# Seven products instead of eight for one more couple of the second mixer's output pair, its weight sums made by VectorE

## The chip, the cores and the metric

The kernel runs on one core of a Trainium2 chip. The metric is device time in microseconds (us), the median of several executions; the profile is one further execution, recorded on the chip. The engines are TensorE (PE, with PEld for its weight loads), VectorE (DVE), ScalarE (ACT), GpSimd (POOL) and SyncE (SP), which here issues nearly all DMA transfers.

## What is computed

A two-layer encoder trunk on 256 tokens of width 2048, all in float32. Each layer is a token mixer and a gated MLP, each behind an RMS norm and added to the residual. The last step of each mixer is a 2048 by 2048 projection; the second mixer's is the one that the change touches:

```python
def hgrn_mixer(hn, w_in, lb, head_g, w_out):
    b, s, _ = hn.shape
    p = hn @ w_in
    ...
    y = head_rmsnorm(y, head_g, B_HEADS) * jax.nn.silu(g)
    return y @ w_out
...
for layer in range(DEPTH):
    hn = rmsnorm(h, norm_mix_g[layer])
    ...
    h = h + mix
    h = h + conv_glu(rmsnorm(h, norm_ffn_g[layer]), ...)
return rmsnorm(h, final_g)
```

## The kernel before

**Precision and products.** Every float32 operand is split in two: a rounded part (wh for weights, the left half of an activation tile) and the rest (wl, the right half). A product of two operands is three matmuls, high by high, high by low and low by high. For weights, ScalarE makes wh by a cast (L146) and VectorE makes wl by a subtraction (L147); both come from a raw tile that SP loads. Weight parts have four buffers each (WB) and, in some stages, two more in another pool (MORE), which every third piece takes by a running counter (`turns["w"]`). An engine works strictly in the order in which its instructions stand, and a scheduler sets that order when the program is built.

**Output projection.** The output of a mixer has four column blocks of 512. `mixed` makes the first (c0), then the two middle ones together (the pair, `two`), then the last (c3). The pair has 16 row tiles of weights, taken two by two: eight couples u = 0 to 7. A couple is a 2 by 2 block product: two halves of the tokens, two row tiles, two column blocks.

**Eight or seven products.** A plain couple needs eight block products, 24 matmuls of 128x512, which accumulate in four banks named pc. A couple in the list SEVEN_MIX is done with seven products (Strassen's scheme in Winograd's form), 21 matmuls, some of which accumulate in four more banks, named mm. That takes four sums of the activations (`token_sums`: tiles f and sx, made by VectorE at L652 and L546, split at L547 and L548) and four sums of the weights (a tile T of 128x1536, and a quarter that is put back into the raw tile). The list is (2, 4, 6) for both mixers.

**Where the weights' sums come from.** In the first mixer they are made on the fly: `combine` issues four VectorE subtractions of 128x512 (L206) one couple ahead. In the second mixer they are made much earlier, while TensorE works on the mixer's input projection, stored to memory (tscr) and loaded back as T (L197) and the last quarter of raw (L198). The tile T has two buffers in a pool that opens only when the mixer's heads are done, since it takes over the heads' memory.

**Order around the change.** The generator `split_squares` yields the pieces of a couple; `squares_by_seven` fetches them some pieces ahead and issues the matmuls; `token` makes the activations' sums of all listed couples as a side job. The mixer's last head is still being finished when the pair begins: its transposes (pz, L1104) are the last readers of the heads' memory.

In the names below, raw_16719 holds couple 1's weights (its halves become wh_16721 and wh_16757), raw_16761 and T_16763 belong to couple 2, and sx_16779 are couple 2's activation sums. yb0 to yb15 are the row tiles of the activations.

Of the kernel before, what the change touches and what calls it, by code (L numbers as in the profile page):

```python
# [8 lines left out]
F32 = mybir.dt.float32  # L9
# [6 lines left out]
P = 128  # L16
T = 256
D = 2048
KT = D // P
# [30 lines left out]
SEVEN = (2, 3, 4, 5, 6, 7, 8, 9), (1, 2, 3, 4, 5, 6, 7)  # L50
# [1 line left out]
SPLIT = (0, 2, 5), (0, 2, 5)  # L52
END = 3
SCRATCH = 4096
SEVEN_MIX = (2, 4, 6)

QUAD = 32
TMS = (0, 4, 8, 11, 15, 18, 21)
# [6 lines left out]
def trunk_kernel(ctx, tc, xT, x_d, fg_d, pp_d, cst_d, w_gate, w_first, w_aq, w_ak, w_av, w_ao, w_aout, w_ao2,  # L65
                 w_bq, w_bv, w_bg, w_bout, w_bo2, w_up, w_d0, w_d1, w_d3, out, mscr, tscr):
    nc = tc.nc
# [114 lines left out]
    def temporary(pool_, name):  # L182
        ff = pool_.name == "ff"
        return pool_.tile([P, 1536], F32, tag="avc" if ff else name, bufs=TEMP if ff else 2, name=name)
# [202 lines left out]
    class Norm:  # L387
# [73 lines left out]
        def x(self, k):  # L461
            side.until(lambda: self.xs[k] is not None)
            return self.xs[k]
# [59 lines left out]
    def project(wsrc, nk, x, norm):  # L523

        def done(c):
            def f_(ps):
                for t in range(2):
                    h = hm[:, t, 512 * c:512 * c + 512]
                    dve.tensor_tensor(h, h, ps[t], ALU.add)
                if norm is not None:  # L530
                    norm.add(c)
            return f_
        return [Chunk("tm", wsrc(c), nk, x, done(c)) for c in range(4)]
# [6 lines left out]
    def token_sums(mp, i, a, b, S, last=None):  # L540

        m = 384 if last else 512
        sx = mp.tile([P, 2 * m], F32R, tag=f"sx{i}", name="sx")
        for i, (x, y, op) in enumerate(((a[:, P:T], b[:, P:T], ALU.add), (a[:, P:T], a[:, 0:P], ALU.subtract),
                                        (S[:, 0:P], a[:, 0:P], ALU.subtract), (b[:, 0:P], S[:, 2 * P:3 * P], ALU.subtract))):
            dve.tensor_tensor(S[:, i * P:(i + 1) * P], x, y, op)  # L546
        act.copy(sx[:, 0:m], S[:, 0:m])  # L547
        dve.tensor_tensor(sx[:, m:2 * m], S[:, 0:m], sx[:, 0:m].bitcast(F32), ALU.subtract)  # L548
        if last:
            act.copy(last[0], S[:, m:512])  # L550
            dve.tensor_tensor(last[1], S[:, m:512], last[0].bitcast(F32), ALU.subtract)
        return [(sx[:, i * P:(i + 1) * P], sx[:, m + i * P:m + (i + 1) * P]) for i in range(m // P)] + ([last] if last else [])

    def pair(src, nk, c0, x, sums, norm, seven):

        def part(t, c):
            o = 512 * (c0 + c)
            return hm[:, t, o:o + 512]

        def mid(ps):  # L560
            P1, P6, P7, P5 = ps
            u = ev.tile([P, 512], F32, tag="jk", bufs=1, name="u")
            act.copy(u, P1)
            dve.tensor_tensor(part(0, 0), part(0, 0), P1, ALU.add)
            dve.tensor_tensor(u, u, P6, ALU.add)
            dve.tensor_tensor(part(0, 1), part(0, 1), P5, ALU.add)
            dve.tensor_tensor(part(0, 1), part(0, 1), u, ALU.add)
            dve.tensor_tensor(part(1, 1), part(1, 1), P5, ALU.add)
            dve.tensor_tensor(u, u, P7, ALU.add)  # L569
            pool.tensor_tensor(part(1, 0), part(1, 0), u, ALU.add)  # L570
            pool.tensor_tensor(part(1, 1), part(1, 1), u, ALU.add)

        def done(ps):
            for c in range(2):
                for t in range(2):
                    h = part(t, c)
                    dve.tensor_tensor(h, h, ps[2 * t + c], ALU.add)
                if norm is not None and c == 0:
                    norm.add(c0)
            if norm is not None:  # L580
                side.push(second())

        def second():
            yield 3.0
            norm.add(c0 + 1)

        ch = Chunk("st", src, nk, x, done)
        ch.mid, ch.seven, ch.sums = mid, seven, sums
        ch.stored, ch.waits, ch.pool, ch.ends, ch.rest = {}, (), None, False, False
        return ch  # L590
# [29 lines left out]
    early = ([], []), ([], [])  # L620
# [6 lines left out]
    def store(ch, src, u, todo):  # L627
        ch.stored[u] = tscr[turns["t"]]
        turns["t"] += 1
        todo.append((src[:, 2048 * u:2048 * (u + 1)], ch.stored[u]))  # L630

    def mixed(w, w2, x, norm, close, layer=None):

        c0, _, _, c3 = project(lambda c: w[c // 3], KT, x, norm)
        op, SX, first = ExitStack(), {}, c0.done

        def sums(u):
            side.until(lambda: u in SX)
            return SX[u]

        two = pair(w2, KT, 1, x, sums, norm, SEVEN_MIX)
        if layer is not None:
            for u in SEVEN_MIX:
                store(two, w2, u, early[layer][0])
            two.waits = [early[layer][1]]

        def token():
            for i, u in enumerate(SEVEN_MIX):
                f = temporary(two.pool, "f")
                for j in range(2):  # L650
                    y = x(2 * u + j).bitcast(F32)
                    dve.tensor_tensor(f[:, j * T:(j + 1) * T], y[:, 0:T], y[:, T:2 * T], ALU.add)  # L652
                SX[u] = token_sums(two.pool, i, f[:, 0:T], f[:, T:2 * T], f[:, 2 * T:4 * T])
                yield 5.0

        def done(ps):
            side.drain()
            close()
            two.pool = op.enter_context(tc.tile_pool(name="op", bufs=1))
            two.pool.tile([P, LEAD], F32, name="lead")  # L660
            first(ps)
            side.push(token())

        c0.done, c3.before = done, op.close
        return [c0, two, c3]


    def mlstm(norm, nxt):
# [270 lines left out]
        def yx(k):  # L939
            side.until(lambda: YT[k] is not None)  # L940
            return YT[k]

        return chunks + mixed(w_aout, w_ao2, yx, nxt, stack.close)


    def hgrn(norm, nxt):
# [196 lines left out]
        def yx(k):  # L1143
            side.until(lambda: YT[k] is not None)
            return YT[k]

        return chunks + mixed(w_bout, w_bo2, yx, nxt, stack.close, 1)


# [182 lines left out]
def build(nc, ins, out_shape=(2, P, D), **kw):  # L1332
    ap = {k: nc.dram_tensor("in_" + k, a.shape, mybir.dt.from_np(a.dtype), kind="ExternalInput").ap()
          for k, a in ins.items()}
    out = nc.dram_tensor("out", out_shape, F32, kind="ExternalOutput").ap()
    mscr = nc.dram_tensor("mscr", (64, T), F32, kind="Internal").ap()
    tscr = nc.dram_tensor("tscr", (len(SEVEN_MIX) + 4 * len(SEVEN[0]) + 4 * len(SEVEN[1]), P, 2048), F32, kind="Internal").ap()
    with tile.TileContext(nc, schedule_with_timeline_sim=True) as tc:  # L1338
        with ExitStack() as ctx:
            trunk_kernel(ctx, tc, ap["xT"], ap["x"], ap["fg"], ap["pp"], ap["cst"], ap["w_gate"], ap["w_first"],  # L1340
                         ap["w_aq"], ap["w_ak"], ap["w_av"],
                         ap["w_ao"], ap["w_aout"], ap["w_ao2"], ap["w_bq"], ap["w_bv"], ap["w_bg"],
                         ap["w_bout"], ap["w_bo2"], ap["w_up"], ap["w_d0"], ap["w_d1"], ap["w_d3"], out, mscr, tscr, **kw)
# [12 lines left out]
```

## Time and profile before

| | us |
|---|---|
| median of three runs | 2373.69 (2372.8 to 2375.37) |
| profiled execution, its own time | 2372.06 |
| its span, first to last instruction | 2370.1 |
| TensorE busy | 2357.5 |
| VectorE busy | 1965.9 |
| ScalarE busy | 1464.1 |
| second mixer's pair, first to last matmul of line 234 | 1600.6 to 1644.2 |

In a timeline a row merges equal instructions that follow each other: start, length of all, engine, line, operation, tiles, count, and in brackets the idle time just before with the instruction that ended it. Matmuls overlap in the pipeline, so the distance from one start to the next is shorter than the listed length of one. The granted clock of TensorE is 0.999 over the span.

### The profile page before, as it was taken

Reading aid. Unit: us, or ns where it says so; the run is one execution under the profiler, and the core shown is the slowest. Engines: PE = TensorE matmul, PEld = TensorE weight load, DVE = VectorE, ACT = ScalarE, POOL = GpSimd, SP = SyncE. Lnnn points to the kernel's source line nnn. Section 1 sums busy time; section 2 is a strip of 40 time slices with the busy share of each in tenths; the row PEclk is TensorE's granted clock in tenths of the full one; section 3 lists DMA queues with packets and bytes.
Section 4 is the critical chain, followed back from the end, with each engine's and each line's share of the span. In section 5 each row is a group of like instructions: output and inputs, shape, how many; then the busy total and the mean of one; then the engine's idle time right before and its main releaser. Section 6 shows DMA issues by size and latency. Waiting matters only on the chain. (4 is left out here: it accounts for less than half of the span.)

```text
span 2370.1 us, 38326 instructions
## 1 busy us (share of the span) xinstructions
PE 2357.5 (99%) x14548; PEld 2019.1 (85%) x14548; DVE 1965.9 (83%) x3028; ACT 1464.1 (62%) x2321; POOL 196.9 (8%) x244
## 2 busy tenths in 40 slices
PE   9999999999999999999999999999999999999998
PEld 8888888888888888888888888888888888888886
DVE  7777687888888898887887888778789888888988
ACT  7655456555565555675777777776555566555565
POOL 0100000000000000000232322220000000000000
PEclk9999999999999999999999999999999999999999
DMA  8776656888988888986666666646788898888896
GB/s 302 237 245 244 214 194 208 295 286 292 317 316 321 308 282 294 351 309 223 211 204 213 218 217 210 207 171 232 265 301 281 293 337 317 288 295 296 318 347 219
DMA packets 121832, 632.96 MB, mean 267 GB/s; under 512 B 13728, under 2 KB 14240, under 8 KB 77232
## 3 DMA queue, kind: packets, MB, share of 16 engines
q1 hardware_dynamic: 119952, 626.51, 75.0%
q0 software_dynamic: 1120, 3.21, 0.8%
q8 instruction: 114, 1.87, 0.3%
q10 hardware_dynamic: 576, 0.79, 0.1%
q14 instruction: 70, 0.57, 0.1%
HBM read 562.24 MB, written 68.22 MB: 266 GB/s over the span
## 5 line engine op out<-in xcount | busy, mean ns | idle before, releaser
L346 PE MATMUL mm<-xt,wh 128*128 128x512 f32 x3776 | 1311.6, 394 | 1.5 <-issue 1.5
L147 DVE TENSOR_TENSOR wl<-raw,wh 128x1024 fp32r<-128x1024 f32 (+1 forms) x844 | 1036.5, 1232 | 247.6 <-ACT wh L146 239.6
L146 ACT CAST wh<-raw 128x1024 fp32r<-128x1024 f32 (+1 forms) x844 | 876.1, 1043 | 528.8 <-PE mm L346 311.3
L350 PE MATMUL mm<-xt,wl 128*128 128x256 f32 x3776 | 1043.0, 278 | 0.0
L346 PEld LDWEIGHTS mm<-xt,wh 128*128 128x128 f32 x3776 | 705.5, 188 | 161.6 <-issue 1.8
L350 PEld LDWEIGHTS mm<-xt,wl 128*128 128x128 f32 x3776 | 709.2, 188 | 5.1 <-issue 0.4
L362 PE MATMUL mm<-wh,xt 128*128 128x512 f32 x1024 | 322.5, 393 | 0.8 <-ACT xt L368 0.6
L234 PE MATMUL pc<-wh,g 128*128 128x512 f32 x776 | 261.9, 390 | 0.0
L362 PEld LDWEIGHTS mm<-wh,xt 128*128 128x128 f32 x1024 | 191.5, 188 | 40.2 <-ACT xt L368 1.1
L611 DVE TENSOR_TENSOR praw<-praw 128x512 f32<-128x512 f32 x252 | 174.8, 694 | 43.7 <-DMA praw<-in_w_d 26.0
L362 PE MATMUL mm<-wl,xt 128*128 128x512 f32 x512 | 198.2, 391 | 0.0
L234 PEld LDWEIGHTS pc<-wh,g 128*128 128x128 f32 x776 | 145.6, 188 | 30.5 <-ACT wh L146 0.2
L234 PE MATMUL pc<-wl,g 128*128 128x512 f32 x388 | 151.0, 389 | 0.0
L234 PE MATMUL mm<-wh,sx 128*128 128x512 f32 x396 | 140.4, 389 | 0.0
L147 DVE TENSOR_TENSOR wl<-T,wh 128x1024 fp32r<-128x1024 f32 (+1 forms) x132 | 126.5, 969 | 12.3 <-ACT wh L146 12.1
L146 ACT CAST wh<-T 128x1024 fp32r<-128x1024 f32 (+1 forms) x132 | 109.6, 836 | 35.9 <-PE mm L234 13.1
L570 POOL TENSOR_TENSOR hm<-hm,u 128x512 f32<-128x512 f32 x10 | 14.8, 1482 | 1221.5 <-DVE u L569 1121.3
L362 PEld LDWEIGHTS mm<-wl,xt 128*128 128x128 f32 x512 | 96.2, 188 | 18.8
L1046 DVE TENSOR_TENSOR QK<-QK,G 128x256 f32<-128x256 f32 x224 | 104.7, 516 | 6.1 <-ACT kq L1025 5.7
L1170 ACT COPY avc<-mm 128x256 f32<-128x256 f32 x172 | 63.9, 372 | 65.8 <-PE mm L350 65.5
L1025 ACT COPY kq<-QK 128x512 f32<-128x512 f32 x112 | 74.5, 669 | 35.7 <-DVE QK L1046 27.8
L234 PEld LDWEIGHTS mm<-wh,sx 128*128 128x128 f32 x396 | 74.3, 188 | 15.4
(237 smaller groups left out, 2218.4 us busy)
## 6 DMA issues: line engine op xcount, KB each, us to landing
raw<-in_w_up SPq DMA_DIRECT2D x172, 1024.0 KB, 6.2
tscr<-praw SPq DMA_DIRECT2D x126, 512.0 KB, 6.7
praw<-in_w_d SPq DMA_DIRECT2D x120, 512.0 KB, 7.1
raw<-in_w_bq SPq DMA_DIRECT2D x48, 1024.0 KB, 5.0
T<-tscr SPq DMA_DIRECT2D x63, 768.0 KB, 8.1
raw<-in_w_d SPq DMA_DIRECT2D x60, 768.0 KB, 6.7
raw<-in_w_ao SPq DMA_DIRECT2D x24, 1024.0 KB, 4.8
raw<-in_w_d SPq DMA_DIRECT2D x24, 1024.0 KB, 7.4
```

Source lines behind the costliest of these rows:

```text
L146: pin(act.copy(wh[:, :m], r))
L147: pin(dve.tensor_tensor(wl[:, :m], r, wh[:, :m].bitcast(F32), ALU.subtract))
L234: pin(pe.matmul(ps, a, b, start=id(ps) not in begun, stop=stop and i == 2))
L346: pe.matmul(ps[f], wh[:, c:c + P], x, start=k + kk == 0, stop=False)
L350: pe.matmul(ps[f][:, 0:T], wl[:, c:c + P], x[:, 0:T], start=False, stop=k + kk == ch.nk - 1)
L362: pe.matmul(ps[t], x[:, a + t * P:a + (t + 1) * P], w[:, c], start=st and i == 0, stop=sp and i == 2)
L570: pool.tensor_tensor(part(1, 0), part(1, 0), u, ALU.add)
L611: dve.tensor_tensor(out, x, y, ALU.subtract)
L1025: act.copy(m, blocks(QK, h))
L1046: dve.tensor_tensor(two[:, j], two[:, j], by[:, j], ALU.mult)
L1170: act.copy(z, p[:, T:2 * T])
```

## The change

The second mixer's list becomes (2, 3, 4, 6); the first mixer's stays. Couple 3 is not stored early: it is named in FLY_MIX, so `combine` makes its weights' sums with VectorE during the pair, as all couples of the first mixer do. The scratch tensor gets one more slot, which nothing uses.

```diff
-SEVEN_MIX = (2, 4, 6)
+SEVEN_MIX = (2, 4, 6), (2, 3, 4, 6)
+FLY_MIX = (3,)
...
         op, SX, first = ExitStack(), {}, c0.done
+        seven = SEVEN_MIX[layer or 0]
...
-        two = pair(w2, KT, 1, x, sums, norm, SEVEN_MIX)
+        two = pair(w2, KT, 1, x, sums, norm, seven)
         if layer is not None:
-            for u in SEVEN_MIX:
-                store(two, w2, u, early[layer][0])
+            for u in seven:
+                if u not in FLY_MIX:
+                    store(two, w2, u, early[layer][0])
             two.waits = [early[layer][1]]

         def token():
-            for i, u in enumerate(SEVEN_MIX):
+            for i, u in enumerate(seven):
```

The program up to the second mixer's pair is the same instruction for instruction on every engine. From the pair on the scheduler orders the engines anew. Line numbers of the changed kernel are higher by one to three.

On ScalarE, this is the queue at the pair's second and third couple before, from the cast of couple 1's first half on (raw_16866 is couple 3's raw tile):

```order
L146 COPY wh_16721<-raw_16719 128x1024
L368 ACTIVATE yb15_16676<-pz_16673,pp_70 128x256
L146 COPY wh_16757<-raw_16719 128x1024
L146 COPY wh_16804<-T_16763 128x1024
L146 COPY wh_16868<-raw_16866 128x1024
L146 COPY wh_16766<-raw_16761 128x1024
L515 ACTIVATE jk_16745,ss8_16744<-hm_75 128x512
L547 COPY sx_16779<-f_16776 128x512
```

And this is the same place in the changed kernel (raw_16804 is now couple 3's raw tile):

```order
L147 COPY wh_16721<-raw_16719 128x1024
L369 ACTIVATE yb15_16676<-pz_16673,pp_70 128x256
L147 COPY wh_16811<-T_16763 128x1024
L147 COPY wh_16873<-raw_16804 128x1024
L147 COPY wh_16757<-raw_16719 128x1024
L147 COPY wh_16766<-raw_16761 128x1024
L147 COPY wh_16815<-raw_16761 128x1024
L516 ACTIVATE jk_16745,ss8_16744<-hm_75 128x512
L548 COPY sx_16779<-f_16776 128x512
```

The cast of couple 1's second half, wh_16757, was first after yb15; it now stands behind the cast of T_16763, which has to be loaded first, and behind a cast for couple 3. The cast of the activation sums sx_16779 moved back by one cast of weights too.

On TensorE, this is the place where couple 1's second half is first used, before:

```order
L234 MATMUL pc_16756<-wh_16687,yb1_11555 128x512
L234 MATMUL pc_16753<-wh_16757,yb3_12367 128x512
L234 MATMUL pc_16754<-wh_16757,yb2_12063 128x512
L234 MATMUL pc_16755<-wh_16757,yb3_12367 128x512
L234 MATMUL pc_16756<-wh_16757,yb2_12063 128x512
L234 MATMUL pc_16753<-wl_16758,yb3_12367 128x512
L234 MATMUL pc_16753<-wh_16757,yb3_12367 128x512
```

The same place in the changed kernel:

```order
L235 MATMUL pc_16756<-wh_16687,yb1_11555 128x512
L235 MATMUL pc_16753<-wh_16757,yb3_12367 128x512
L235 MATMUL pc_16754<-wh_16757,yb2_12063 128x512
L235 MATMUL pc_16755<-wh_16757,yb3_12367 128x512
L235 MATMUL pc_16756<-wh_16757,yb2_12063 128x512
L235 MATMUL mm_16749<-wh_16766,yb4_13286 128x512
L235 MATMUL mm_16750<-wh_16811,sx_16779 128x512
L235 MATMUL mm_16750<-wl_16812,sx_16779 128x512
L235 MATMUL mm_16751<-wh_16811,sx_16779 128x512
L235 MATMUL mm_16751<-wl_16812,sx_16779 128x512
L235 MATMUL mm_16752<-wh_16815,sx_16779 128x512
L235 MATMUL pc_16753<-wl_16758,yb3_12367 128x512
```

Up to the four matmuls with wh_16757 nothing moved; behind them six matmuls of couple 2, five of which use sx_16779, now come ahead of those with wl_16758.

On VectorE, between the rest of yb15 and wl_16758 stood only six small sums of f and the two additions to hm. Now two subtractions of couple 3 (L207), wl_16812, wl_16874, a third subtraction and the like number of small sums stand between them, and one subtraction of couple 3 stands ahead of yb15, so that all four come before wl_16758. Behind wl_16758 follow wl_16767, wl_16816 and then the rest of sx_16779.

On SP, the load of couple 4's T now stands behind three more transfers and waits until T_16763 is used up, since couple 3's own sums take the second buffer of T. Because the running counter of weight pieces is two higher after the pair, the second layer's MLP pairs put other pieces in the two additional buffers, and the scheduler orders them a little differently too; the number of operations there is the same.

More of the change, by code (lines that the diff above doesn't have):

```diff
@@ L1336, in build @@
     mscr = nc.dram_tensor("mscr", (64, T), F32, kind="Internal").ap()
-    tscr = nc.dram_tensor("tscr", (len(SEVEN_MIX) + 4 * len(SEVEN[0]) + 4 * len(SEVEN[1]), P, 2048), F32, kind="Internal").ap()
+    tscr = nc.dram_tensor("tscr", (len(SEVEN_MIX[1]) + 4 * len(SEVEN[0]) + 4 * len(SEVEN[1]), P, 2048), F32, kind="Internal").ap()
     with tile.TileContext(nc, schedule_with_timeline_sim=True) as tc:
```

## Prediction

> **What bounds the kernel now.** I read the page first, then the waits of TensorE, then the timelines of the second mixer's pair. On the page, the line of busy times says that TensorE has nearly no idle time to lose:
>
> ```profile
> PE 2357.5 (99%) x14548; PEld 2019.1 (85%) x14548; DVE 1965.9 (83%) x3028; ACT 1464.1 (62%) x2321; POOL 196.9 (8%) x244
> ```
>
> All waits of TensorE in the span, longest first (us in total, times, longest):
>
> ```profile
> PE mm L346 <- issue: 1.5, 1, 1.5
> PE idle L1239 <- POOL ones L1232: 1.1, 1, 1.1
> PE mm L362 <- ACT xt L368: 0.6, 1, 0.6
> PE pc L234 <- DVE wl L147: 0.4, 1, 0.4
> ```
>
> The span of 2370.1 us is TensorE's work, 3.6 us of waits and an end behind the last matmul. A change can gain only by taking matmuls away, and any new wait of TensorE is paid in full, since no later wait is there to swallow it. The one wait in line 234 lies in the pair that is changed. TensorE's timeline there:
>
> ```profile
> 1607.22 0.62 PE L362 MATMUL mm<-wh,yb 128*128 128x512 f32 x2
> ...
> 1608.81 1.36 PE L234 MATMUL pc<-wh,yb 128*128 128x512 f32 x5
> 1610.53 0.50 PE L234 MATMUL pc<-wl,yb 128*128 128x512 f32 x1 [0.36 <-DVE wl L147]
> 1610.86 0.39 PE L234 MATMUL pc<-wh,yb 128*128 128x512 f32 x1
> ...
> 1618.60 1.07 PE L234 MATMUL pc<-wh,yb 128*128 128x512 f32 x4
> 1619.51 0.39 PE L234 MATMUL mm<-wh,yb 128*128 128x512 f32 x1
> ```
>
> Four matmuls from 1618.60 to 1619.51 make 0.228 us for one from start to start. The five from 1608.81 are the last with couple 1's first half and the four with its second, wh_16757, so those four start at 1608.81 + 0.23 = 1609.04; the wait behind them is for wl_16758.
>
> **What the change takes away.** Couple 3 goes from 24 matmuls to 21: 3 times 0.228 is 0.68 us less on TensorE. It lies on the path, so all of it counts. That is the whole gain: 0.03% of the time, where about 0.2% (4.75 us) is what a measurement of this kernel can tell from no change.
>
> **What it adds, as work.** VectorE's rows in the pair and, for the subtractions of weights, in the first mixer's pair:
>
> ```profile
> 332.05 0.68 DVE L206 TENSOR_TENSOR T<-raw 128x512 f32<-128x512 f32 x1
> 332.65 1.22 DVE L147 TENSOR_TENSOR wl<-raw,wh 128x1024 fp32r<-128x1024 f32 x1
> ...
> 1604.66 1.43 DVE L652 TENSOR_TENSOR f<-yb 128x256 f32<-128x256 f32 x4 [2.94 <-PE pz L1104]
> 1606.01 0.28 DVE L546 TENSOR_TENSOR f<-f 128x128 f32<-128x128 f32 x1
> 1606.22 0.48 DVE L369 SCALAR_TENSOR_TENSOR yb<-pz,pp,yb 128x256 fp32r<-128x256 f32 x1
> 1606.61 1.09 DVE L546 TENSOR_TENSOR f<-f 128x128 f32<-128x128 f32 x5
> 1607.65 0.69 DVE L529 TENSOR_TENSOR hm<-hm,mm 128x512 f32<-128x512 f32 x1
> 1608.25 0.29 DVE L546 TENSOR_TENSOR f<-f 128x128 f32<-128x128 f32 x1
> ...
> 1611.69 2.36 DVE L147 TENSOR_TENSOR wl<-raw,wh 128x1024 fp32r<-128x1024 f32 x2
> ...
> 1635.30 2.36 DVE L147 TENSOR_TENSOR wl<-raw,wh 128x1024 fp32r<-128x1024 f32 x2 [3.56 <-ACT wh L146]
> ```
>
> From start to start a 128x512 operation takes 0.60 us (332.05 to 332.65), a sum of f from yb 0.34 (four in 1.35), a small sum 0.21, a wl of 1024 columns 1.14 (2.36 less one of 1.22). So VectorE gets four subtractions (2.4), two f (0.7), four small sums (0.8), the rest of sx (0.6) and the wl of T, 1.14 and about 0.6: 6.2 us. ScalarE gets casts of T, 0.96 and some 0.5, and of sx, some 0.5. Against this stands VectorE's free time by stages (us; busy PE, PEld, DVE, ACT, POOL; clock, DMA):
>
> ```profile
> 323.50:351.50 28.00, 28.00 (x125) 23.21 (x124) 26.52 (x33) 17.95 (x22) 0.00 (x0) 1.00 0.57 196
> 1604.60:1631.80 27.20, 26.84 (x119) 21.73 (x118) 25.93 (x41) 18.84 (x25) 0.00 (x0) 1.00 0.78 279
> 1631.80:1635.30 3.50, 3.50 (x17) 2.92 (x16) 0.00 (x1) 1.09 (x2) 0.00 (x0) 1.00 0.89 304
> ```
>
> In the first 27.2 us VectorE has 1.3 us free, then it idles through 3.5 us, because it ran ahead: 4.8 us for 6.2. By the sum alone TensorE would end up 1.4 us late. The first mixer's pair, in the first row, does three couples on the fly at 26.5 of 28.0 us with TensorE at 28.0 of 28.0. I take nothing for the work, because the wait worked out next gives VectorE more time than it lacks.
>
> **What it moves: the term that decides.** ScalarE at this place:
>
> ```profile
> 1604.66 0.47 ACT L368 ACTIVATE yb<-pz,pp 128x256 fp32r<-128x256 f32 x1 [4.20 <-PE pz L1104]
> 1607.87 1.06 ACT L146 CAST wh<-raw 128x1024 fp32r<-128x1024 f32 x1 [2.73 <-PE mm L362]
> 1609.47 1.05 ACT L146 CAST wh<-T 128x1024 fp32r<-128x1024 f32 x1 [0.55 <-DMA T<-tscr]
> 1610.43 2.00 ACT L146 CAST wh<-raw 128x1024 fp32r<-128x1024 f32 x2
> 1612.33 0.62 ACT L515 ACTIVATE jk<-hm 128x512 f32<-128x512 f32 x1
> ...
> 1612.95 0.60 ACT L547 CAST sx<-f 128x512 fp32r<-128x512 f32 x1
> ```
>
> And the transfer it waits for: SP's row, and the time to landing of the three loads of T in this pair (least, median, most); then the medians of raw loads of the same size here, and of all loads of T:
>
> ```profile
> 1604.71 0.80 SPq L197 DMA_DIRECT2D T<-tscr  x2
> ...
> DMA to landing us min/median/max: 4.7/6.1/6.1
> ...
> raw<-in_w_bo SPq DMA_DIRECT2D x3, 768.0 KB, 4.3
> ...
> T<-tscr SPq DMA_DIRECT2D x63, 768.0 KB, 8.1
> ```
>
> Today wh_16757 is cast at 1607.87, as soon as TensorE frees its buffer, ends at 1608.93, and TensorE takes it at 1609.04. In the new order the cast of T_16763 stands ahead of it. That tile's load cannot be issued before 1604.71: it waits for the head's transposes, which end there, and nothing of that changes. It lands 4.7 us later, so ScalarE stands still until 1609.47 with wh_16757, wh_16766, wh_16815 and sx_16779 queued behind.
>
> Then, with 0.96 us from cast to cast (1609.47 to 1610.43): T 1609.47, couple 3's raw 1610.43, wh_16757 1611.39, ended at 1612.44. TensorE waits from 1609.04 to about 1612.49, which is 3.45 us. Its four matmuls last until 1613.40; wh_16766 (started 1612.35) ends at that time, and its one matmul runs until 1613.68. The next needs sx_16779: wh_16815 starts at 1613.31, the squares of hm (L516) at 1614.27, sx 0.62 later at 1614.89, ending at 1615.49. TensorE goes on at 1615.54, a second wait of 1.86 us. That is the sixth matmul from 1609.04 on; the sixth starts today at 1610.86, with the 0.36 us wait ahead of it, which goes since wl_16758 is wanted later. So TensorE is 4.68 us later.
>
> Is VectorE ready by then? From 1604.66: two f, a subtraction, two f, a small sum, yb15 (0.39) and a small sum end at 1607.43; a subtraction, three small sums, two hm, a subtraction and two small sums at 1610.88; wl_16812 and wl_16874 at 1613.16, a subtraction and a small sum at 1613.97. So wl_16758 ends at 1615.19. TensorE wants it five matmuls after 1615.54, at 1616.68: 1.5 us in hand. The rest of sx_16779, three wl later, ends at 1618.1 and is wanted some four us after that. yb15 comes 0.6 us later than now, 0.1 us late for c0's last matmuls; the wait that follows swallows it.
>
> The sum: 4.68 less 0.68 is 4.0 us. The profiled execution took 2372.06 us (2370.1 of span and 2.0 around it), which makes 2376.1. The median of the runs shown, 2373.69, is 1.6 above that execution, so I forecast 2377.7. Only the landing of T is uncertain here, and it enters one to one: by the raw loads, 4.3 us, the change costs 3.6; by the other two of T, 6.1 us, 5.4. I take 4.7, because it is the same transfer released by the same matmul. The median of all loads, 8.1, is from stages with more traffic.
>
> **Rivals.** (1) No new wait: the cast of T does not hold up wh_16757, for instance because the two loads of T shared the engines and one alone lands much sooner. Only the 0.68 us would remain, 2373.0. It would take a landing by about 1606, 1.3 us after issue, and the least shown is 4.3.
>
> (2) The waits let TensorE's clock fall. In these rows the last matmul starts at 2360.93 and lasts 0.39, and the clock column then goes from 1.00 to 0.50; the row with 1.5 us of TensorE idle, around 1226, keeps 1.00:
>
> ```profile
> 2360.93 0.39 PE L234 MATMUL pc<-wh,g 128*128 128x512 f32 x1
> ...
> 1226.00:1228.00 2.00, 0.54 (x4) 0.22 (x3) 1.46 (x6) 1.70 (x6) 0.00 (x0) 1.00 0.77 320
> 2364.00:2366.00 2.00, 0.00 (x0) 0.00 (x0) 1.11 (x2) 1.03 (x2) 0.00 (x0) 0.80 0.37 136
> 2366.00:2368.00 2.00, 0.00 (x0) 0.00 (x0) 0.00 (x0) 0.00 (x0) 0.00 (x0) 0.50 1.03 371
> ```
>
> A mean of 0.80 says the fall came 1.2 us into 2364 to 2366, so 3.9 us after the last matmul ended. The new wait, about 3.3 us without a matmul running, lies between 1.5 and 3.9, nearer to the upper. If the clock falls and takes as long to come back as it took to fall, half of 3.9 us of matmuls is lost: 1.9 us, 2379.6. [...]
>
> (3) A second wait later in the pair. Couple 4's T is now loaded only when T_16763 is used up, which VectorE reaches, after 1613.97, behind three wl (3.4), two rests of sx (1.2), four f (1.4), four small sums (0.8) and one wl of 512 columns (0.6), at 1621.4; TensorE wants its cast 63 matmuls after 1615.54, at 1629.9, so a landing of up to 7.3 us is hidden. At 8.1 it is 0.8 us late, and a second such miss in the reordered pairs of the second layer's MLP would cost as much: 1 to 2 us, 2379.2. Against it: those pairs show no wait of TensorE today.
>
> **How the numbers follow.** The forecast has 0.56, and a third of that lies beyond 4.75 us, towards a landing of 6.1; the clock 0.19, the second wait 0.16, no new wait 0.06, and a gain that I do not see 0.03. Slower by over 0.2%: 0.19 + 0.19 + 0.16 = 0.54. Within 0.2%: 0.37 + 0.06 = 0.43. Faster: 0.03. The forecast's own bounds are 2377.3 to 2379.1; with the clock on top of the later landing 2381.0, and with the medians of either kernel uncertain by 1 us, the range is 2375.5 to 2381.5.
>
> **What would show it.** Right: a wait of TensorE in line 235 for ScalarE's wh of about 3.4 us and one for sx of 1.9, and ahead of them ScalarE idle for the load of T into 1609.5. Wrong: no wait above 1 us there, a TensorE clock below 1.00 behind it (rival 2), or a wait on T of couple 4 near 1630 (rival 3).

## The result: slower by 0.27%, and the profile after

The changed kernel takes 2379.28 us (median of 9 runs, 2378.62 to 2381.97), the kernel before 2372.80 beside it (9 runs). The ratio is 1.0027, with a 95% interval of 1.0018 to 1.0036. The forecast was 2377.7 in a range of 2375.5 to 2381.5, with a chance of 0.54 for slower. The profiled execution of the changed kernel took 2378.62 us with a span of 2376.5, against 2372.06 and 2370.1 before.

The waits of TensorE in the changed kernel, longest first (us in total, times, longest):

```profile
PE pc L235 <- ACT wh L147: 2.4, 1, 2.4
PE mm L235 <- ACT sx L548: 1.6, 1, 1.6
PE mm L347 <- issue: 1.5, 1, 1.5
PE mm L363 <- ACT xt L369: 1.2, 1, 1.2
...
PE pc L235 <- DVE wl L148: 1.0, 1, 1.0
PE mm L363 <- ACT wh L147: 0.5, 1, 0.5
```

Three of its waits lie behind the start of the pair and are not in the kernel before: the two that the prediction named, for wh and for sx, and a third for a wl, in the second layer's MLP. (The waits in lines 347 and 363 lie ahead of the pair, where the two programs are the same.) ScalarE's timeline at the pair's second couple shows where the first two come from:

```profile
1604.98 0.47 ACT L369 ACTIVATE yb<-pz,pp 128x256 fp32r<-128x256 f32 x1 [4.20 <-PE pz L1107]
1609.21 1.05 ACT L147 CAST wh<-T 128x1024 fp32r<-128x1024 f32 x1 [3.75 <-DMA T<-tscr]
1610.16 3.88 ACT L147 CAST wh<-raw 128x1024 fp32r<-128x1024 f32 x4
...
1614.57 0.60 ACT L548 CAST sx<-f 128x512 fp32r<-128x512 f32 x1
```

SP's queue has the load that the cast of T waits for:

```profile
1605.04 0.33 SPq L198 DMA_DIRECT2D T<-tscr  x1
```

ScalarE stands still for 3.75 us, until T is there 4.2 us after its issue, with couple 1's second half behind it. TensorE's timeline at the same place:

```profile
1609.41 0.40 PE L235 MATMUL pc<-wh,yb 128*128 128x512 f32 x1
1612.20 1.20 PE L235 MATMUL pc<-wh,yb 128*128 128x512 f32 x4 [2.39 <-ACT wh L147]
1613.24 0.41 PE L235 MATMUL mm<-wh,yb 128*128 128x512 f32 x1
1615.28 0.76 PE L235 MATMUL mm<-wh,sx 128*128 128x512 f32 x1 [1.63 <-ACT sx L548]
1615.84 0.63 PE L235 MATMUL mm<-wl,sx 128*128 128x512 f32 x1
1616.26 0.63 PE L235 MATMUL mm<-wh,sx 128*128 128x512 f32 x1
...
1618.37 0.39 PE L235 MATMUL pc<-wl,yb 128*128 128x512 f32 x1
```

Seven matmuls from 1615.28 to 1618.37 take 3.09 us, 0.40 to 0.56 each from start to start, where 0.228 is usual. Busy time by stretches (PE, PEld, DVE, ACT, POOL, then the granted clock of TensorE, DMA share and GB/s), with borders where the clock falls and rises, tells why:

```profile
1608.08:1611.49 3.41, 1.73 (x8) 1.06 (x6) 3.41 (x10) 2.28 (x3) 0.00 (x0) 1.00 0.07 27
1611.49:1614.90 3.41, 1.45 (x5) 0.86 (x5) 3.41 (x5) 3.41 (x6) 0.00 (x0) 1.00 0.00 0
1614.90:1618.31 3.41, 3.04 (x7) 2.48 (x8) 3.41 (x5) 1.41 (x4) 0.00 (x0) 0.50 0.53 153
```

The clock was halved from 1614.90 to 1618.31, for 3.41 us. At the full clock the seven matmuls take 1.60, so this cost 1.49 us. The fall came during the second wait: the 3.41 us ahead of it hold 0.71 us of the first wait, 1.45 us of matmuls and 1.25 us of the second wait.

The third wait is in the second layer's first MLP pair. TensorE, VectorE and GpSimd there:

```profile
1979.19 0.50 PE L235 MATMUL pc<-wl,g 128*128 128x512 f32 x1 [0.96 <-DVE wl L148]
```

```profile
1974.86 4.28 DVE L148 TENSOR_TENSOR wl<-raw,wh 128x1024 fp32r<-128x1024 f32 x2
```

```profile
1974.51 1.30 POOL L571 TENSOR_TENSOR hm<-hm,u 128x512 f32<-128x512 f32 x1 [296.18 <-PE pc L235]
1975.76 2.29 POOL L572 TENSOR_TENSOR hm<-hm,u 128x512 f32<-128x512 f32 x1
```

Two wl take 4.28 us together, where two in the pair take 2.36, while GpSimd adds to hm beside them.

To say where the time went, I cut TensorE's timeline at five points: the starts of the first pc of the second mixer's pair, of the first mm<-xt,wh of the second MLP, of its first pc<-wh,g and of the first pc<-wh,g of its second round, and the end of the last matmul. Before, these are at 1600.60, 1668.97, 1914.54, 2256.32 and 2361.32. The table gives what each stage takes more (us) in the profiled executions, beside the difference of the medians of the runs from those of the kernel before on the same chip (the interval of the ratio, times 2372.5):

| kernel | up to the pair | pair and last block | feed-forward stage | MLP, first round | MLP, second round | median over before (95%) |
|---|---|---|---|---|---|---|
| changed | 0.3 | **4.93** | 0.00 | **1.26** | -0.11 | 6.5 (4.3 to 8.5) |
| e9_swap_in_before | -0.9 | 3.39 | -0.01 | 0.01 | -0.11 | 4.5 (1.9 to 6.2) |
| e7_warm | -1.5 | 3.51 | 0.00 | 0.58 | -0.11 | 4.8 (2.6 to 6.9) |
| e3_counter_back | -0.3 | 6.27 | 0.00 | 0.00 | -0.10 | 5.7 (3.3 to 7.6) |
| e2_counter | 0.9 | 0.00 | -0.01 | 0.91 | 1.33 | -0.7 (-2.6 to 1.7) |
| e1_ordered | 0.6 | 3.22 | 4.35 | 2.07 | -0.11 | 7.5 (4.7 to 10.2) |
| e1_again | -1.1 | 3.22 | 4.36 | 0.62 | -0.10 | one run |
| e6_sums_later | 0.6 | 2.49 | 0.00 | 2.28 | -0.11 | 3.5 (1.4 to 5.7) |
| e8_all | 0.8 | 1.66 | 0.00 | 0.00 | -0.10 | 1.2 (-0.2 to 4.0) |
| e5_stored_back | 0.8 | 1.40 | 4.36 | 0.04 | 1.07 | 6.7 (4.0 to 9.0) |
| e10_sums_first | -1.4 | 3.52 | 4.35 | 0.04 | 1.73 | 7.4 (4.7 to 10.4) |

The first column is the spread of single executions: up to the pair nearly all these programs are the same. So the columns behind it are what to compare, and these too come from single executions: e1_ordered and e1_again are one program, and their first MLP rounds differ by 1.45 us. In the changed kernel the pair's 4.93 is 4.09 of waits up to the sixth matmul after 1609, less 0.68 of matmuls saved, plus 1.49 of slow clock (4.90).

### The profile page after: what moved, and what is told of

Its sections match the earlier page's. It is cut to its first block, busy times and chain, and to the rows that moved or that the text cites. A ratio compares the mean times of both kernels' runs of the same rounds, so it can differ in the third digit from the quotient of the medians.

```text
span 2376.5 us, 38336 instructions
## 1 busy us (share of the span) xinstructions
PE 2358.4 (99%) x14545; PEld 2018.3 (85%) x14545; DVE 1974.2 (83%) x3041; ACT 1464.6 (62%) x2324; POOL 197.1 (8%) x244
```

## Experiments

The edits are shown shortened, in their deciding lines.

**The order alone, in the kernel before.** Theory A says that the time goes to ScalarE's order, theory B that it goes to VectorE's work on the sums. The first experiment has the order without the work: one edge makes ScalarE cast T first.

```diff
+# u == 2, after the parts of T have been issued; held_back is couple 1's second cast
+tc.add_manual_dep(held_back.ins, casts[-1].ins.name, <order only>)
```

> The kernel before, eight couples as they were (three by seven products, all from stored sums), with one thing altered: ScalarE casts T of couple 2 ahead of couple 1's second half. No operation is added or taken away. Theory A: T lands 4.2 to 4.7 us after its issue at 1604.7, its cast takes 0.96, so couple 1's second half is cast by 1611.0 to 1611.5 and TensorE waits 2.0 to 2.5 us for it, and then about as long for its wl as today (0.36): 2375 to 2375.5; a clock that falls behind the wait would add 1.5. Theory B (VectorE's sums are the cost): no change, 2372.8.

Measured: 2376.27, 4.5 over before; 3.39 in the pair. TensorE's timeline, then its clock:

```profile
1607.88 0.39 PE L242 MATMUL pc<-wh,yb 128*128 128x512 f32 x1
1610.48 1.84 PE L242 MATMUL pc<-wh,yb 128*128 128x512 f32 x4 [2.22 <-ACT wh L146]
1612.12 0.63 PE L242 MATMUL pc<-wl,yb 128*128 128x512 f32 x1
```

```profile
1607.38:1610.79 3.41, 1.19 (x5) 0.68 (x5) 2.30 (x6) 2.35 (x3) 0.00 (x0) 1.00 0.56 229
1610.79:1614.20 3.41, 3.41 (x9) 2.50 (x8) 3.41 (x4) 3.41 (x6) 0.00 (x0) 0.50 0.39 85
```

With no operation more, moving one cast ahead makes a wait of 2.22 us and halves the clock for 3.41 us. Theory A is shown to be enough by itself: the wait in place of the 0.36 before is 1.86 longer, and the remaining 1.5 of the 3.39 fit the slow clock.

**The clock alone.** Theory C says that the waits let the clock fall and that this costs 1.5 us. Ten matmuls that nobody reads fill the first wait of the changed kernel.

```diff
+if ch.warm and u == 1:
+    for _ in range(10):
+        pe.matmul(P7, <yb0>, <couple 0's wl>, start=True, stop=True)
```

> The changed kernel with ten more matmuls of 128x512 ahead of couple 1's second half, into a bank that is begun anew afterwards: 2.3 us of TensorE work inside the wait of 2.39 us, whose result nobody reads. Theory C (the waits let the clock fall, which costs 1.5 us): the clock column stays at 1.00 from 1614 to 1618, the seven matmuls after the second wait take 1.6 us in place of 3.1, and the time is 2377.8. Rival (the fall comes from the second wait alone, or costs nothing): 2379.3; if the ten matmuls are not hidden, up to 2381.6.

Measured: 2376.54, 4.8 over before; the pair 3.51 over before, 1.42 less than in the changed kernel. TensorE's timeline and clock:

```profile
1607.83 2.43 PE L315 MATMUL mm<-wl,yb 128*128 128x512 f32 x10
1610.45 1.20 PE L235 MATMUL pc<-wh,yb 128*128 128x512 f32 x4 [0.19 <-ACT wh L147]
...
1613.52 0.47 PE L235 MATMUL mm<-wh,sx 128*128 128x512 f32 x1 [1.62 <-ACT sx L561]
1613.83 0.39 PE L235 MATMUL mm<-wl,sx 128*128 128x512 f32 x1
```

```profile
1611.38:1614.79 3.41, 1.79 (x9) 1.28 (x8) 3.41 (x6) 3.17 (x7) 0.00 (x0) 1.00 0.12 16
```

The second wait is still there, 1.62 us long, and the clock stays at 1.00. So the second wait alone did not bring the fall here; in the changed kernel it came with 0.71 us of the first wait in the same 3.41 us. The 1.42 us saved are close to the 1.49 of the matmuls' pace.

**The counter.** The third new wait lies in the MLP. The pool of every third weight piece hangs on a counter that couple 3 raises by two. One kernel sets it back in the changed kernel, one raises it in the kernel before.

```diff
 yield from split_squares(ch, parts)
+turns["w"] += ch.turn        # -2 in e3_counter_back, +2 in e2_counter
```

> The changed kernel with the counter that picks the pool of every third wh and wl (turns["w"]) set back by the two that couple 3 adds, right after the second mixer's pair; nothing else. Theory D (the counter's shift reorders the pairs of the second layer's MLP and makes the wait of 0.96 us for a wl near 1979): that wait goes, and the time falls by about 1.1 us to 2378.2, with the waits in the output pair as they were. Rival (the wait comes from the later start alone): 2379.3.

> The kernel before, with nothing altered but the counter that picks the pool of every third wh and wl: raised by two after the second mixer's output pair, as couple 3's two more parts do in the changed kernel. Theory D (that shift alone makes the wait in the second layer's MLP): a wait of about 1 us of TensorE for a wl between 1970 and 1985, and 1.0 to 1.3 us over the kernel before. Rival (it takes the changed pair ahead of it as well): no change.

Measured: e3 2377.45, 5.7 over before; e2 2372.51, no difference that the runs can tell. In e3 the first MLP round takes as long as before (0.00 over it). VectorE's two stretched wl, beside the same two additions of GpSimd, are these there:

```profile
1976.18 2.03 DVE L148 TENSOR_TENSOR wl<-raw,wh 128x1024 fp32r<-128x1024 f32 x1
1978.13 2.32 DVE L148 TENSOR_TENSOR wl<-T,wh 128x1024 fp32r<-128x1024 f32 x1
```

The wl are as long beside GpSimd in this place too, 4.27 us from the start of the first to the end of the second where two in the pair take 2.36, but at a moment when TensorE is not waiting for them. The same holds in the kernel before, where the two take 2.04 and 2.32 us (at 1970.07 and 1972.03). So what is new in the changed kernel is not the long wl but the order in which the pieces come. In e2 the counter alone brings the wait into the kernel before, at the same place:

```profile
1974.43 0.50 PE L235 MATMUL pc<-wl,g 128*128 128x512 f32 x1 [0.57 <-DVE wl L147]
```

Over all profiles with the counter raised, the first MLP round takes 0.58 to 2.28 us longer (six of six), and over all with it unmoved or set back 0.00 to 0.04 (five of five, the profile before aside). So theory D, that the counter's shift makes the wait in the MLP, stands on the profiles. The medians of e2 and e3 alone would not carry it, since an effect of 1 us lies inside their intervals. The pair of e3 is 1.34 longer than that of the changed kernel, and its clock stayed at half for twice as long. The two programs have the same orders up to the MLP, so this differs by execution:

```profile
1610.16:1613.57 3.41, 1.45 (x5) 0.86 (x5) 3.41 (x7) 3.41 (x5) 0.00 (x0) 1.00 0.00 0
1613.57:1620.40 6.83, 5.68 (x14) 4.46 (x14) 6.83 (x14) 2.18 (x6) 0.00 (x0) 0.50 0.68 224
```

**The order put right.** Now the changed kernel with ScalarE's order of before: edges chain the casts, and the rests on VectorE, of couples 1 to 3.

```diff
+keep_order = (cast_chain, rest_chain) if ch.ordered and 1 <= u <= 3 else <free>
-yield *parts(r[:, 0:1024], 1024, more=ch.pool), 1
+yield *parts(r[:, 0:1024], 1024, keep_order, ch.pool), 1
```

> The changed kernel with the casts and rests of couples 1 to 3 of the second mixer's output pair held in the order in which they are written; couple 3's sums still stand on VectorE where the change puts them. Theory A (the time goes to ScalarE's order, the cast of T ahead of the cast of couple 1's second half): TensorE's waits of 2.39 us for wh and 1.63 us for sx go, and the clock stays at 1.00. What is left is VectorE: with a subtraction and the f of one couple more ahead of it, the wl of couple 1's second half ends near 1612.3, and TensorE, which wants it near 1610.5, waits 1.5 to 2 us. With 0.68 us of matmuls saved and about 1.1 us lost later in the MLP: 2374.0 to 2375.5. Theory B (the sums on VectorE are the cost, the order of the casts is not): within 1 us of the changed kernel's 2379.3.

Measured: 2379.21, 7.5 over before, where theory A expected 1 to 3. The total looks like theory B's, but the stages say otherwise. First, the pair:

```profile
1612.71 0.49 PE L250 MATMUL pc<-wl,yb 128*128 128x512 f32 x1 [1.42 <-DVE wl L162]
...
1628.07 0.50 PE L250 MATMUL pc<-wh,yb 128*128 128x512 f32 x1 [0.93 <-ACT wh L161]
```

The waits for the first cast and for sx are gone and the clock stays up, but TensorE waits for a wl of VectorE instead, later for a wh, and loses 3.22 in the pair. The wh stands behind a cast that waits for a load of T:

```profile
1624.55 1.57 ACT L161 CAST wh<-T 128x1024 fp32r<-128x1024 f32 x2 [0.92 <-DMA T<-tscr]
```

This is couple 4's T. Its load was issued at 1618.70, when VectorE had made its last rest of couple 2's T, and took 5.83 us to land. Second, the feed-forward stage behind it takes 4.35 us longer without any wait. TensorE's groups of instructions from 1700 to 1900, before and in this kernel (last columns: busy us, mean ns of one, idle):

```profile
L346 PE MATMUL mm<-xt,wh 128*128 128x512 f32 x578 | 200.4, 394 | 0.0
L350 PE MATMUL mm<-xt,wl 128*128 128x256 f32 x578 | 160.1, 277 | 0.0
```

```profile
L362 PE MATMUL mm<-xt,wh 128*128 128x512 f32 x567 | 200.4, 399 | 0.0
L366 PE MATMUL mm<-xt,wl 128*128 128x256 f32 x566 | 159.0, 281 | 0.0
```

In the same 200 us there are 567 matmuls of 128x512 for 578, 1.9% fewer, at a clock of 1.00. From start to start they run in a fixed cycle of three, 241, 236 and 233 ns, where before each takes 230 to 233. Was that the execution or the kernel? The same program was profiled once more.

> e1_ordered once more, unchanged, for its profile alone. If the 249.9 us of the second layer's feed-forward stage (245.6 in the others) belong to the kernel, they come again to 0.1 us; if they belonged to that execution, the stage takes 245.6. The waits in the output pair (1.42 us for wl, 0.93 for wh) should repeat within 0.2 us.

Measured: the stage takes 4.36 over before again, the pair 3.22 again, the wait for wl 1.42 again. It belongs to the kernel. In the pair the order put right saves 1.71 us (4.93 to 3.22, alike in both profiles); the medians, less the 4.35, are too uncertain to say more. What is left comes from VectorE's work, directly in the wl and by way of the late load in the wh. So theory B has its part: with ScalarE's order right, VectorE's work alone costs nearly as much as ScalarE's order alone does in e9 (3.22 for 3.39). In the changed kernel the one hides the other, so that only the first is seen.

**The sums later, and all together.** In e6, with the order of e1, couple 3's four subtractions stand behind the rest of couple 2's second half; e8 also sets the counter back.

```diff
-if u + 1 in ch.seven and u + 1 not in ch.stored:
+fly = u + 1 in ch.seven and u + 1 not in ch.stored
+if fly and ch.ordered:
+    raw(u + 1)                           # the load alone
+elif fly:
     combine(u + 1)
...
+if fly and ch.ordered:                   # behind the second half of couple u
+    combine(u + 1, rest_chain)
```

> The changed kernel with two things altered in the second mixer's output pair: the casts and rests of couples 1 to 3 in the order in which they are written (as in e1_ordered), and couple 3's four sums on VectorE behind the rest of couple 2's second half, so that nothing stands ahead of couple 1's rests that does not stand there before the change. If the cause is what stands ahead of couple 1's second half on ScalarE and on VectorE, both at once: no wait above 0.5 us between 1609 and 1616, the clock at 1.00, and the pair costs between 0.7 us less and 0.7 us more than before; the counter's shift still adds 1.26 in the MLP, so 0.6 to 2 us over the kernel before. Rival (VectorE has too much to do in the whole pair, wherever the sums stand): the waits only move towards 1625 to 1632, the pair stays 3 us longer as in e1_ordered, and the time is 4 us over the kernel before.

> As e6_sums_later, and the counter that picks the pool set back by two after the pair (as in e3_counter_back). If the two theories hold, the MLP of the second layer takes as long as before and the whole is 0.7 us faster to 0.7 us slower than the kernel before. Rival (VectorE too full in the whole pair): 3 us slower than before.

Measured: e6 2376.71, 3.5 over before; e8 2374.37, 1.2 over before, a ratio of 1.0008 (0.9999 to 1.0017), which is not told apart from the kernel before. The waits up to 1616 are gone, and one comes later. TensorE, ScalarE and VectorE in e8, and the busy times of the stretch that was shown for the kernel before:

```profile
1618.88 0.39 PE L256 MATMUL pc<-wh,sx 128*128 128x512 f32 x1
1620.57 0.73 PE L256 MATMUL mm<-wh,sx 128*128 128x512 f32 x2 [1.30 <-ACT wh L161]
1621.25 0.50 PE L256 MATMUL pc<-wl,yb 128*128 128x512 f32 x1
```

```profile
1619.47 1.05 ACT L161 CAST wh<-T 128x1024 fp32r<-128x1024 f32 x1 [3.21 <-DVE T L222]
```

```profile
1619.90 0.69 DVE L222 TENSOR_TENSOR T<-raw,T 128x512 f32<-128x512 f32 x1
```

```profile
1605.35:1632.55 27.20, 25.80 (x109) 19.29 (x107) 27.14 (x50) 19.23 (x26) 0.00 (x0) 1.00 0.61 214
```

VectorE is busy for 27.14 of 27.20 us (25.93 before) and TensorE for 25.80 (26.84 before): in this stretch VectorE has become the bound. The pair costs 1.66, between the theory's bound (0.7) and the rival's 3; in e6, where every engine has the same order up to the MLP, it costs 2.49, since ScalarE waits 1.74 us for a late load of T there (0.87 in e8) and TensorE 0.50 us for the wh.

**Is it VectorE's order or its time?** In e8 the activation sums of couples 4 and 6 stand between the subtractions. Here they stand behind them.

```diff
+while two.ordered and i >= 2 and two.summed is None:
+    yield 1.0                            # f of couples 4 and 6 after the sums
```

> As e8_all, and the f sums of couples 4 and 6 (six operations each, 1.5 us together on VectorE ahead of the last subtraction in e8_all) behind couple 3's four subtractions. In e8_all the cast of couple 3's T waits for the last subtraction until 1619.4 and TensorE waits 1.30 us for that cast. Theory (VectorE has enough time in the pair as a whole, only its order is wrong): the sums end 1.2 us earlier, that wait goes, and the pair takes 0.3 us less to 0.3 us more than before. Rival (VectorE lacks the time): the wait comes back behind couple 3, the pair stays 1 to 1.7 us longer than before. A second question: the second layer's feed-forward stage behind the pair ran 4.35 us longer than in all the others, at a full clock and without waits, in e1_ordered and e5_stored_back alone. In this kernel that stage's wh, wl and accumulators lie in the same buffers as in e1_ordered. If the buffers decide it, the stage is 4.3 us longer here too and the time is 4 us over the kernel before; if it was chance, it takes the 245.6 us of the others.

Measured: 2380.02, 7.4 over before; the pair 3.52. TensorE's timeline:

```profile
1622.16 0.50 PE L257 MATMUL pc<-wl,yb 128*128 128x512 f32 x1 [0.34 <-DVE wl L162]
1625.64 0.50 PE L257 MATMUL pc<-wl,yb 128*128 128x512 f32 x1 [0.58 <-DVE wl L162]
1627.38 0.50 PE L257 MATMUL pc<-wl,yb 128*128 128x512 f32 x1 [0.54 <-DVE wl L162]
```

The wait of 1.30 us is gone and several small ones for wl have come in its place, more in all. The theory fails: this order moves the wait and makes it larger, beyond the 1 to 1.7 us of the rival too. That VectorE lacks the time in any order is likely, with 27.14 of 27.20 us busy in e8, but only these orders were tried. On the second question, the feed-forward stage is 4.35 longer, as expected from the buffers; no trace shows the buffers themselves.

**No sums in the pair.** Last, couple 3's sums made early and stored, like those of the other three, with the counter set back.

```diff
-FLY_MIX = (3,)
+FLY_MIX = ()
```

> Four couples by seven products, but couple 3's sums made early and stored like those of the other three, so that VectorE makes none in the pair; the counter set back by two as in e3_counter_back. Leaves the casts of couple 1 ahead of that of T, as in the kernel before. If VectorE's sums and the order that goes with them are the whole cost: the pair takes 0.68 us less than before, the rest the same, so 0.7 us faster than the kernel before, provided that the earlier sums (0.75 MB more written and read, and four subtractions) are hidden in the stage ahead, which TensorE bounds. Rival (seven products for this couple cost more than they save in any form, for instance through ScalarE's two more casts or couple 3's T landing late): 1 us slower or more, with a wait for wh or wl in the pair.

Measured: 2379.84, 6.7 over before, of which 4.36 is again the feed-forward stage. The pair is 1.40 over before, not 0.68 under it:

```profile
1625.70 0.50 PE L236 MATMUL pc<-wh,yb 128*128 128x512 f32 x1 [0.48 <-ACT wh L147]
...
1627.60 0.50 PE L236 MATMUL pc<-wh,yb 128*128 128x512 f32 x1 [0.44 <-ACT wh L147]
```

Two waits for wh and some smaller ones near 1625 eat more than the three matmuls give, even without the subtractions. So the rival holds (what keeps ScalarE late there was not followed): in none of these forms does couple 3 by seven products pay, and none of the kernels beats the kernel before. The 1.1 to 1.7 us that e2, e5 and e10 lose in the MLP's second round were not followed further.

## Why the prediction was right, and where it was not

- **The deciding term**, the cast of T ahead of couple 1's second half, was right in its place and its cause: e9_swap_in_before makes it alone. Its size was 4.09 at the sixth matmul for a forecast 4.68, because T's cast started 4.17 us after the load's issue for 4.76 assumed. The time was read off a profile in which two loads of T were issued together; the change holds the second back, as the text ahead of the prediction says. In the eight profiles with one load it lands after 4.07 to 4.21 us, in the four with two after 4.45 to 4.66. So rival 1 was right that one load alone lands sooner, but this is worth 0.6 us and not the whole wait; that the two loads share the engines was its own guess and is not shown. The first wait is listed with 2.39 for 3.45: beside the earlier landing, TensorE reached it 0.27 late (1609.64, for 1609.04 and 0.33 of a later start), where 0.1 had been expected from the later yb15. The second is listed with 1.63 for 1.86; counted from start to start it is 1.81.
- **The gain** of 0.68 us is in the sum as forecast.
- **VectorE's work at nothing** held for the changed kernel: no wait in its pair ends on VectorE. The reason held too, for when the wait is taken away (e1_ordered, e8_all) the lack appears. It is larger than the 1.4 us of the sum: in e8 the pair is 1.66 over before with 0.68 saved, so 2.3. I had counted free time over the pair as a whole, but TensorE wants each piece at its own moment.
- **Rival 2, the clock**, was given 0.19 as an alternative, and came on top of the forecast: 1.49 us for 1.9 priced. The step that failed is the threshold: I had taken a fall to need one wait near 3.9 us, from a single fall at the end of the profile before. In the twelve profiles that last fall comes 2.40 us (e1_again) to 5.30 us (e7) after the last matmul, so 3.9 was chance. What the traces have in common is a grid. In the changed kernel, e9 and e3 the last fall comes 757.76 us behind the first, which is 222 steps of 3.413 us, and the slow stretches are one step long, or two in e3. In the step ahead of a fall TensorE was idle for 1.96 us in the changed kernel and in e3, for 2.22 in e9 and 2.40 in e1_again. Steps with 1.62 us idle (e7), 1.68 (the changed kernel, up to 1611.49) and 1.74 (e8, up to 1228.75) kept the clock, and so did this one at the end of e7, with 1.88 us idle:

```profile
2362.31:2365.72 3.41, 1.53 (x7) 0.94 (x5) 1.98 (x6) 0.04 (x1) 0.09 (x1) 1.00 0.76 273
```

A wait of 2.00 us in e1_ordered, from 1226.5 to 1228.5, kept the clock too: a border of the grid, counted back from the last fall there as in e7 and e8, cuts it in two at 1227.90. So in these runs the clock fell when 1.96 us or more of a step were idle, in one wait or in two, and not at 1.88 us or less. The ends of matmuls are modelled, so that border is rough. Where a wait lay on the grid was part of its price here: 2.00 us across a border kept the clock in e1_ordered, and 1.96 us within one step were followed by the slow stretch that cost 1.49 us in the changed kernel.
- **Rival 3** came in its second half, a miss in the reordered MLP pairs, at 1.26 for 1 to 2 us. Its first half did not come: TensorE has no wait for couple 4's T. (In e1_ordered, where the first two waits are gone, it does come.) The cause of the miss was not a late load of T, as I had it, but the wl that run beside GpSimd (two in 4.28 us, for 2.36 in the pair) and are wanted sooner in the new order (a wait of 0.96 us).
- **The total**: 2376.1 forecast for the profiled execution, less 0.59 on the waits, plus 1.49 for the clock, 1.15 in the MLP, 0.32 up to the pair and 0.16 around the span is the measured 2378.62. The median came out 1.6 above the forecast, inside the range. That is in part luck: the forecast adds its 4.0 us to the 2373.69 of three runs, and the nine runs of the kernel before give 2372.80. Beside that the change cost 6.5 us for a forecast 4.0. The miss is that the two rivals were priced as cases of their own, though nothing in them excluded the forecast or each other.

## What to carry to other kernels

On an engine that works in strict order, an operation that waits for a load must not stand ahead of one whose data are there (here ScalarE stood still for 3.75 us, and TensorE then waited 2.39 us); when a scheduler reorders a queue, look first for such a swap. When a wait is long, ask at once what the clock does behind it, and add the price (1.49 us in the changed kernel) to the wait instead of weighing one against the other. Saving 0.68 us on TensorE is not worth 6 us of VectorE work in a stretch where VectorE is at 95% (25.93 of 27.20 us in the kernel before): the lack showed as soon as ScalarE's order was put right (the pair 3.22 us over before in e1_ordered).

## What the runs showed of the hardware

- TensorE's clock fell to half at steps of 3.41 us, when 1.96 us or more of the step ahead had been idle (1.96 in the changed kernel and e3, 2.22 in e9, 2.40 in e1_again), and kept full speed after steps with up to 1.88 us idle. It stayed at half for one step (changed kernel, e9) or two (e3).
- A load of T alone landed after 4.07 to 4.21 us (eight profiles), and with a second one issued 0.4 us behind it after 4.45 to 4.66 (four).
- In e8 a listed wait cost TensorE more than its length: around the wait of 1.30 us, the matmul behind it starts 1.69 us after the one ahead (0.23 is usual), and it and the next take 0.34 each from start to start: 1.46 and 0.22, together 1.68 us lost.
- A VectorE wl of 1024 columns, 1.22 us alone, takes 2.03 and 2.32 us beside GpSimd's additions of 128x512 in e3, and the two of the changed kernel 4.28 together.
- A stage of 245.6 us took 1.8% longer, at a clock of 1.00 and without waits, in e1_ordered (twice), e5_stored_back and e10_sums_first, each time by 4.35 or 4.36 us; in e1_ordered its 128x512 matmuls ran in a cycle of three lengths (241, 236 and 233 ns). By the programs as built, e10 has its weight parts and accumulators in the same buffers as e1, and was expected to be slow for that reason alone. So I take the placement in the buffers, or something that goes with it, for the cause. No trace shows it, and what about it matters stays open.
